# The mixing branches of a two-layer decoder step as stopping routines between the large products

## The chip, the cores and the metric

The kernel runs on one core of one Trainium2 chip. The metric is the device time of one execution in microseconds. Five engines work side by side, each through its own list of instructions in order: PE (TensorE, the matmuls), DVE (VectorE), ACT (ScalarE), POOL (GpSimd) and SP (SyncE, which here only issues DMA transfers). They wait for one another by semaphores. Matmuls write to eight PSUM banks; DVE and ACT read the banks out.

## What is computed

One inference step of a trunk of two layers. The rows (columns of x in the kernel) are 8 sequences of 4 new tokens with past state, and one prompt of 16 meta and 512 further tokens. Per layer:

```python
x = x + 0.5 * swiglu(rmsnorm(x, ffn1_norm), ffn1_w_in, ffn1_w_out)
h = rmsnorm(x, mix_norm)
fq, fk, fv, ff, sz, sxbc, sdt, gq, gk, gv, glr, gg = split(h @ w_mix_in)
# FoX: softmax attention on normalised q and k, bias = sums of log forget gates
# SSD: causal conv over x, B, C; state space recurrence in chunks of 128; gate silu(z); grouped norm
# GLA: linear attention with a decay per key channel from a low-rank gate; norm; swish gate
x = x + concat(fox_o, ssd_o, gla_o) @ w_mix_out
x = x + 0.5 * swiglu(rmsnorm(x, ffn2_norm), ffn2_w_in, ffn2_w_out)
```

The prompt attends causally to itself; the 8 sequences attend to 512 past tokens each, in pages of 128 that a page table names. New keys, values, gates and states are returned too.

## The kernel before

x lies in SBUF with 1024 features on 8 x 128 partitions and 560 columns. Group A is 304 columns (tile 4: 32 sample and 16 meta columns; tiles 0 and 1: 128 prompt columns each), group B 256 (tiles 2 and 3). Every large product is float32 by three terms: activations and weights are split into a high and a low part (`hhiA`, `hloA`, `whi`, `wlo`; A or B is the group), and `mm3` issues high x high, low x high and high x low for each of 8 pieces of the contraction: 24 matmuls in a row. `unit` fetches a 128 x 1024 piece of weights by a DMA on SP into one of three `raw` buffers, splits it in two halves on ACT (`whi`) and DVE (`wlo`, every fifth on POOL); there are four buffers of each.

A layer is ffn1, mix, ffn2. The two ffn parts are long rows of products. `mix` holds the rest: projections (`gla_in`, `fox_in`, `ssd_in`, per group), then for each tile the routines `gla_tile`, `ssd_tile`, `fox_tile`, for the sample columns `fox_decode` with 64 paged keys and values per layer, `fox_norm` for q and k, `fox_meta` (layer 0 only), then `split_o` (the branches' output O into high and low), `mix_out` (8 products per group and the sum into x) and the norm. In a tile, small matmuls alternate with steps on DVE, ACT and POOL. `ssd_tile` begins with products on `da`, transposes of the conv outputs `xc`, products of `s` (c_tri times dr) with c_strict, forms the weights `s` from them, multiplies them with the inputs, updates the state `Ssd` by a product with `sbt`, and at its end normalises y, with a diagonal matrix `dg` from ACT on the one side of a matmul, into O. The tiles of one branch hang on one another by the state.

The order in which the instructions are written decides on each engine's order. In `mix` it is a string, `MIX_ORDER` (line 162): every word calls the next stretch, up to a `yield`, of a projection, a tile's routine as a whole, a split, a part of `mix_out`. The scheduler of the framework then lets small matmuls slip between products where it sees room. `after(n, f)` delays a closure until n more products have been written. PSUM: 2 banks `psg` for products, 3 `psL` for GLA and SSD, 3 `psF` for FoX and the rest.

Of the kernel before, what the change touches and what calls it, by code (L numbers as in the profile page):

```python
# [173 lines left out]
BUFS = {"s1": 5, "f2": 3, "g2": 8, "s2": 5, "pg": 9}  # L174
# [58 lines left out]
class Trunk:  # L233
    def __init__(self, tc, a, es):
# [11 lines left out]
        self.pending = []  # L246
        self.nlo, self.lo_pool = 0, 0
# [23 lines left out]
    def mm(self, out, lhsT, rhs, start=True, stop=True, **k):  # L271
        return self.T.matmul(out, lhsT, rhs, start=start, stop=stop, **k)  # L272

    def tr(self, out, in_):
        p = in_.shape[0]
        self.T.transpose(out, in_, self.c("ident")[:p, :p])  # L276
# [157 lines left out]
    def mm3(self, out, parts):  # L434

        n = len(parts)
        for i, ((wh, wl), (xh, xl)) in enumerate(parts):
            self.mm(out, wh, xh, start=i == 0, stop=False)
            self.mm(out, wh, xl, start=False, stop=False)
            last = self.mm(out, wl, xh, start=False, stop=i == n - 1)  # L440
        self.tick(last)

    def after(self, n, f):

        self.pending.append([n, f])

# [206 lines left out]
    def fox_in(self, l, H):  # L653
# [20 lines left out]
        yield  # L674
        qa = self.qaug
        pst = self.ps(self.psF)
        for name in ("fk0", "fk1", "fq0", "fq1"):
            if name == "fq0":
                yield
            w = self.unit(self.a["wfm"][l, FMI[name]])  # L680
            isq, hp = name[1] == "q", int(name[2])
            for g in GRP:
# [8 lines left out]
                def sums(g=g, sq=sq, i=i, last=name == "fq1" and g == "B"):  # L691
                    for j, (ti, c0, tn) in enumerate(TILES[g]):
                        o = 8 * j + i + (24 if g == "B" else 0)
                        self.mm(pst[:, o:o + 2], sq[:, c0:c0 + 128], self.c("fsel"))
                    if last:
                        for h in GRP:
                            o, nt = 24 if h == "B" else 0, len(TILES[h])
                            self.V.tensor_scalar(self.R[h]["fst"][:, :nt, :], pst[:, o:o + 8 * nt].rearrange("p (j i) -> p j i", j=nt),
                                                 EPS, None, op0=ALU.add)
# [4 lines left out]
    def gla_in(self, l, g, H):  # L704
        R, n, nt = self.R[g], GRP[g][1], len(TILES[g])
        gin = self.g2(128 * nt).rearrange("p (j c) -> p j c", j=nt)
        pt = self.ps(self.psF)

        def use(j, ti, c0, tn, ps):
# [6 lines left out]
            self.tr(pt[:, 128 * j:128 * j + 128], gv[:, 0:128])  # L716

        self.tok_unit(l, 0, g, H, use)
        gt = self.g2(128 * nt)
        self.act(gt, pt[:, :128 * nt])  # L720
        pg = self.ps(self.psF)
        for j in range(nt):
            self.mm(pg[:, 128 * j:128 * j + 128], gt[:, 128 * j:128 * j + 128], self.wgate)
        self.tt(gin, pg[:, :128 * nt].rearrange("p (j c) -> p j c", j=nt), self.row["gb"].unsqueeze(1).to_broadcast([128, nt, 128]), ALU.add)
        self.log_sigmoid(gin.rearrange("p j c -> p (j c)"), self.g2(128 * nt), self.g2(128 * nt))
        gh = R["gh"] = self.t([128, 384], "gh", F32R)[:, :128 * nt].rearrange("p (j c) -> p j c", j=nt)
        gl = R["gl"] = self.t([128, 384], "gl", F32R)[:, :128 * nt].rearrange("p (j c) -> p j c", j=nt)
        self.act(gh, gin)
        self.tt(gl, gin, gh.bitcast(F32), ALU.subtract)
        yield  # L730
# [3 lines left out]
        yield  # L734
        for name in ("gg0", "gg1"):
# [3 lines left out]
            self.stt(t[:, :n], t[:, :n], 1.0, ps, ALU.add, ALU.mult)  # L739

    def ssd_in(self, l, g, H):
# [24 lines left out]
        for f in (4, 5, 0, 1, 2, 3):  # L766
            if f in (4, 1):
                yield
            self.conv(l, g, f, self.fm_unit(l, f"c{f}", g, H))
        yield  # L770
        self.tok_unit(l, 3, g, H, lambda *a: use(*a, half=1))

# [46 lines left out]
    def fox_norm(self, l, g):  # L819
# [7 lines left out]
        for j, (ti, c0, tn) in enumerate(tiles):  # L827
            e = self.f2(512)
            self.act(e.rearrange("p (h d) -> p h d", h=8), y[:, j, :].unsqueeze(2).to_broadcast([128, 8, 64]))
            ps = self.ps(self.psF)  # L830
# [26 lines left out]
        for j in range(3):  # L857
            self.tt(lw[:, 1, 4 * j + 4:4 * j + 8], lw[:, 1, 4 * j:4 * j + 4], lw[:, 0, 4 * j:4 * j + 4], ALU.add)
        ps = self.ps(self.psF)
# [26 lines left out]
    def diag(self, r, n):  # L886

        d = self.t([128, 128], "dg", bufs=2)[:n, :n]
# [3 lines left out]
    def fox_tile(self, g, i, c0):  # L892

        R = self.R[g]
# [3 lines left out]
        po = self.ps(self.psF)  # L898
        for hp in range(2):
            ets = []  # L900
            for h in (2 * hp, 2 * hp + 1):
# [16 lines left out]
                dg = self.diag(sums[:, 0:1], 128)  # L918
                pt = self.ps(self.psF)
                for k in range(i + 1):  # L920
                    o = 16 + 128 * k
                    self.mm(pt[:, 128 * k:128 * k + 128], e[0][:, o:o + 128] if o < nk else e[1], dg)
                et = self.f2(kc)
                self.V.tensor_copy(et, pt[:, :kc]) if h % 2 else self.act(et, pt[:, :kc])

# [3 lines left out]
                self.act(emt, pm[:, :128]) if h % 2 else self.V.tensor_copy(emt, pm[:, :128])  # L929
                ets.append((et, emt))  # L930

            for k in range(i + 2):
                for h2, (et, emt) in enumerate(ets):
                    d = slice(128 * hp + 64 * h2, 128 * hp + 64 * h2 + 64)
                    o = po[64 * h2:64 * h2 + 64, 128 * hp:128 * hp + 128]
# [123 lines left out]
    def ssd_tile(self, l, g, j, ti, c0, n):  # L1059
# [122 lines left out]
        if ti == 3:  # L1182
            self.store("ossmp", l, self.Ssd)
# [380 lines left out]
```

## Time and profile before

| | |
|---|---|
| time, median of 3 runs | 2401.96 us (2398.37 to 2403.77) |
| the profiled execution | 2399.53 us, its span 2397.4 us |
| mean granted clock of PE | 0.994 |
| PE busy | 2338.7 us (98%), 18041 matmuls |
| DVE / ACT / POOL busy | 1221.3 / 869.3 / 516.4 us |
| mix of layer 0 | 429.7 to 800.1 us |
| mix of layer 1 | 1622 to 1995 us |
| loaded from HBM | 219.47 MB, 95 GB/s over the span |

Times in the profile are microseconds from the start of the span. A row of instructions names engine, line, operation, output <- inputs and shape; L272 is the matmul helper, L276 the transpose, L279 a two-operand step, L282 one with a scalar besides, L285 an activation or copy on ACT. A wait is put down to the engine and tile that released it. Matmuls overlap in the pipeline, so their pace is the distance of their starts, not their duration. PEclk is the granted clock as a share of 2.4 GHz.

### The profile page before, as it was taken

What the parts mean: (1) busy time and instruction counts of PE and PEld (TensorE: products, weight loads), DVE (VectorE), ACT (ScalarE), POOL (GpSimd) and SP (SyncE); (2) the same over time, 40 slices, a digit from 0 to 9 for tenths busy, and PEclk for the clock granted to TensorE, in tenths of its full rate; (3) what the DMA queues carried; (4) which work ended last, traced back from release to release, by engine and by line L of the source; (5) the groups of instructions that cost most, each with busy time, mean ns of one, the idle gap of its engine ahead of it and who ended that gap; (6) DMA issues with size and microseconds to landing.
All of it is one profiled execution on the core that took longest, in us unless ns stands there. A gap on an engine that the chain in (4) does not pass through costs nothing.

```text
span 2397.4 us, 45049 instructions
## 1 busy us (share of the span) xinstructions
PE 2338.7 (98%) x18041; PEld 2251.5 (94%) x18041; DVE 1221.3 (51%) x2610; ACT 869.3 (36%) x1892; POOL 516.4 (22%) x696
## 2 busy tenths in 40 slices
PE   8999999999999999999999999999998999999999
PEld 8999999987788999999999999999877889999999
DVE  6434444477787633333353333344877975333333
ACT  5323223444455432322343232235444554323231
POOL 4202112334232310100131010113333323101010
PEclk9999999999999999999999999999999999999999
DMA  4222223335332322222322222233442323222222
GB/s 150 90 89 83 85 89 106 86 105 170 102 99 68 115 89 82 87 88 85 92 73 87 88 83 86 88 98 95 120 157 92 98 77 114 88 89 87 89 86 86
DMA packets 89762, 230.25 MB, mean 96 GB/s; under 512 B 12834, under 2 KB 38130, under 8 KB 89554
## 3 DMA queue, kind: packets, MB, share of 16 engines
q1 hardware_dynamic: 89122, 227.22, 30.5%
q8 instruction: 142, 2.33, 0.4%
q14 instruction: 66, 0.54, 0.1%
q10 hardware_dynamic: 432, 0.16, 0.0%
HBM read 219.47 MB, written 7.85 MB: 95 GB/s over the span
## 4 chain that ended last, share of the span: by engine, by line
PE 86%; DVE 7%; POOL 3%; ACT 2%; issue 2%; DMA 1%; POOLq 0%; DVEq 0%; ACTq 0%
PE ps L272 85%; DVE s L282 1%; POOL s L279 1%; DVE g L279 1%; DVE s L279 1%; PE ps L276 1%; DVE wlo L279 1%; DMA raw<-wout 1%; ACT s L285 1%; POOL gst L317 0%; POOL hloA L279 0%; DVE qaug L282 0%; ACT hhiA L285 0%; ACT whi L285 0%; DVE kaug L282 0%
## 5 line engine op out<-in xcount | busy, mean ns | idle before, releaser
L279 DVE TENSOR_TENSOR wlo<-raw,whi 128x512 fp32r<-128x512 f32 (+1 forms) x649 | 459.9, 711 | 400.7 <-ACT whi L285 391.0
L285 ACT ACTIVATE whi<-raw 128x512 fp32r<-128x512 f32 (+1 forms) x680 | 426.4, 630 | 609.3 <-PE ps L272 558.8
L272 PE MATMUL ps<-hhiA,whi 128*128 128x304 f32 (+1 forms) x1664 | 503.4, 303 | 0.0
L272 PE MATMUL ps<-hloA,whi 128*128 128x304 f32 (+1 forms) x1664 | 502.6, 302 | 0.0
L272 PE MATMUL ps<-hhiA,wlo 128*128 128x304 f32 (+1 forms) x1664 | 501.2, 301 | 0.0
L272 PE MATMUL ps<-hhiB,whi 128*128 128x256 f32 x1664 | 471.0, 283 | 3.7 <-ACT s L285 2.3
L272 PE MATMUL ps<-hhiB,wlo 128*128 128x256 f32 x1664 | 471.5, 283 | 1.9 <-DVE wlo L279 1.9
L272 PE MATMUL ps<-hloB,whi 128*128 128x256 f32 x1664 | 468.5, 282 | 0.0
L272 PEld LDWEIGHTS ps<-hhiB,whi 128*128 128x128 f32 x1664 | 315.4, 190 | 6.3 <-ACT s L285 4.3
L272 PEld LDWEIGHTS ps<-hhiB,wlo 128*128 128x128 f32 x1664 | 315.6, 190 | 3.2 <-DVE wlo L279 2.7
L272 PEld LDWEIGHTS ps<-hloA,whi 128*128 128x128 f32 x1664 | 314.2, 189 | 3.3 <-issue 2.4
L272 PEld LDWEIGHTS ps<-hloB,whi 128*128 128x128 f32 x1664 | 314.8, 189 | 1.9 <-issue 1.2
L272 PEld LDWEIGHTS ps<-hhiA,whi 128*128 128x128 f32 x1664 | 313.5, 188 | 1.8 <-issue 1.5
L272 PEld LDWEIGHTS ps<-hhiA,wlo 128*128 128x128 f32 x1664 | 313.7, 189 | 1.3 <-issue 0.8
L279 POOL TENSOR_TENSOR hidA<-s,hidA 128x304 fp32r<-128x304 f32 (+1 forms) x88 | 75.9, 863 | 824.4 <-ACT hidA L285 824.0
L272 PE MATMUL ps<-hidA,whi 128*128 128x304 f32 (+1 forms) x1072 | 223.4, 300 | 0.0
L282 DVE SCALAR_TENSOR_TENSOR x<-ps,x 128x304 f32<-128x304 f32 (+2 forms) x192 | 85.5, 447 | 233.8 <-PE ps L272 232.1
L272 PE MATMUL ps<-hidB,whi 128*128 128x256 f32 x1072 | 193.9, 281 | 0.0
L272 PEld LDWEIGHTS ps<-hidA,whi 128*128 128x128 f32 x1072 | 173.6, 188 | 0.0
L272 PEld LDWEIGHTS ps<-hidB,whi 128*128 128x128 f32 x1072 | 166.2, 189 | 0.0
L272 PE MATMUL ps<-hidA,wlo 128*128 128x304 f32 (+1 forms) x536 | 161.0, 300 | 0.0
L279 DVE TENSOR_TENSOR s<-s,ps 128x256 f32<-128x256 f32 (+4 forms) x194 | 89.9, 464 | 136.1 <-PE ps L272 127.7
(337 smaller groups left out, 3546.4 us busy)
## 6 DMA issues: line engine op xcount, KB each, us to landing
raw<-win SPq DMA_DIRECT2D x176, 512.0 KB, 3.5
raw<-wout SPq DMA_DIRECT2D x64, 512.0 KB, 3.5
raw<-wfm SPq DMA_DIRECT2D x48, 512.0 KB, 3.5
raw<-wmo SPq DMA_DIRECT2D x32, 512.0 KB, 3.6
raw<-wout SPq DMA_DIRECT2D x32, 384.0 KB, 3.4
pg<-kpage SPq DMA_DIRECT2D x64, 130.0 KB, 2.4
pg<-vpage SPq DMA_DIRECT2D x64, 128.0 KB, 2.2
raw<-wtm SPq DMA_DIRECT2D x8, 544.0 KB
```

The lines of the kernel that those rows point to most:

```text
L272: return self.T.matmul(out, lhsT, rhs, start=start, stop=stop, **k)
L276: self.T.transpose(out, in_, self.c("ident")[:p, :p])
L279: return (eng or self.V).tensor_tensor(out=out, in0=a, in1=b, op=op)
L282: return self.V.scalar_tensor_tensor(out=out, in0=a, scalar=s, in1=b, op0=op0, op1=op1)
L285: return self.S.activation(out, in_, f, **k)
```

## The change

`MIX_ORDER` goes. The projections are written in the order gla_in A, fox_in, ssd_in A, gla_in B, ssd_in B. Tiles become generators that `yield` an estimated number of microseconds at each point where PE would wait for another engine. Three lanes (G: GLA tiles 4, 0, 1, then 2, 3; S: SSD likewise; F: fox_norm, decode, FoX tiles 0, 1, meta, 2, 3) hold them. `mm` and `tr` count an estimated PE time in `now`; after each half of a product and each product, `step` advances the lanes that are due, and issues what they write behind that product. The closing products of an SSD or GLA tile go to a list of `ends`, due 7 or 6 us later. `finish` runs lanes without products between where a later stage needs it: S ahead of ssd_in B until tile 1 has its weights, G ahead of gla_in B until tile 1's state is there, and everything at the end. `mix_out` of A is now one piece with the rest of tiles 2 and 3 beside it, then B is split and its products follow, and norm A comes after B's first two.

PSUM banks: `psL` has 6 and `psF` is the same pool. Of smaller things: FoX tiles 0 to 2 put the meta columns' product into the bank of the others, and one copy takes all; FoX's output is copied per pair of heads; the gate's transposes in gla_in go tile by tile, each behind the next product; SSD's diagonal has a tag `ds` of its own and both are made ahead; GLA's `kr` has its own buffer; page buffers are 8 for 9. The core of the diff, with some parts cut:

```diff
-MIX_ORDER = """
-fox_in:A fox_in:A ssd_in:A fox_in:A gla_in:A gla_in:A O:A gla_in:A fox_norm:A fox_norm:B gla:4 decode:A fox:0
-fox:4 gla:0 gla:1 fox:1 ssd_in:A ssd_in:A ssd_in:A ssd:4 ssd:0 ssd:1 gla_in:B gla_in:B gla_in:B ssd_in:B
-ssd_in:B ssd_in:B ssd_in:B split:A O:B gla:2 fox:3 ssd:2 gla:3 out:A out:A fox:2 ssd:3 out:A split:B out:A
-out:B norm:A out:B out:B out:B norm:B
-"""
+STAGES = ("glaA", "fox", "ssdA", "glaB", "ssdB")
+
+LANES = {"G": {"A": (4, 0, 1), "B": (2, 3)}, "S": {"A": (4, 0, 1), "B": (2, 3)}, "F": (0, 1, 4, 2, 3)}
...
-BUFS = {"s1": 5, "f2": 3, "g2": 8, "s2": 5, "pg": 9}
+BUFS = {"s1": 5, "f2": 3, "g2": 8, "s2": 5, "pg": 8}
...
     def mm(self, out, lhsT, rhs, start=True, stop=True, **k):
+        n = int(np.prod(rhs.shape[1:]))
+        self.now += n / 2400 + 0.0125 if rhs.dtype == F32R else max(0.111, n / 1200)
         return self.T.matmul(out, lhsT, rhs, start=start, stop=stop, **k)
...
             last = self.mm(out, wl, xh, start=False, stop=i == n - 1)
+            if i == n // 2 - 1:
+                self.step(last)
         self.tick(last)
+        self.step(last)
...
+    def step(self, last):
+
+        for lane in list(self.lanes.values()):
+            if lane["q"] and lane["due"] <= self.now:
+                with self.tc.issue_after(last.ins):
+                    self.advance(lane)
+        for e in [e for e in self.ends if e[0] <= self.now]:
+            if e[1] in self.O:
+                self.ends.remove(e)
+                with self.tc.issue_after(last.ins):
+                    e[2]()
+
+    def advance(self, lane):
+
+        g = lane["q"][0]
+        try:
+            lane["due"] = self.now + next(g)
+        except StopIteration:
+            lane["q"].pop(0)
+            lane["due"] = self.now
+
+    def end(self, g, wait, f):
+
+        self.ends.append((self.now + wait, g, f))
+
+    def finish(self, names, until=lambda: False):
+
+        while not until():
+            lanes = [self.lanes[n] for n in names if self.lanes[n]["q"]]
+            if not lanes:
+                break
+            lane = min(lanes, key=lambda v: v["due"])
+            self.now = max(self.now, lane["due"])
+            self.advance(lane)
...
-            self.tr(pt[:, 128 * j:128 * j + 128], gv[:, 0:128])
+
+            def turn():
+                pt = self.ps(self.psF)
+                self.tr(pt[:, :128], gv[:, 0:128])
+                self.act(gt[:, 128 * j:128 * j + 128], pt[:, :128])
+
+            self.after(1, turn)
...
         for f in (4, 5, 0, 1, 2, 3):
-            if f in (4, 1):
-                yield
             self.conv(l, g, f, self.fm_unit(l, f"c{f}", g, H))
-        yield
+        self.branch("S", [self.ssd_tile(l, g, *a) for i in LANES["S"][g] for a in self.tile_of(g, i)], 5.0)
         self.tok_unit(l, 3, g, H, lambda *a: use(*a, half=1))
+        R["zz"] = True
...
+            yield 3.0
+            while g not in self.O:
+                yield 1.0
+
+            po = self.ps(self.psF)
...
-        self.act(self.O[g][:, 0:2, self.ocols(g, c0, 128)[0]], po[:, 0:256].rearrange("p (a b) -> p a b", a=2))
+            self.act(self.O[g][:, hp, self.ocols(g, c0, 128)[0]], po[:, 0:128])
...
+        while "zz" not in R:
+            yield 1.0
...
-        pt = self.ps(self.psL)
-        for g2 in range(2):
-            dg = self.diag(r[:, g2:g2 + 1], n)
-            for f in (2 * g2, 2 * g2 + 1):
-                self.mm(pt[:, f * n:(f + 1) * n], y[:, 128 * f:128 * f + 128], dg)
+        dgs = [self.diag(r[:, g2:g2 + 1], n, "ds") for g2 in range(2)]
...
+        self.end(g, 7.0, turn)
...
+        for w in STAGES:
+            if w == "fox":
+                self.fox_in(l, H)
+            elif w[:3] == "ssd":
+
+                if w[3] == "B":
+                    self.finish("S", lambda: ("S", 1) in self.done)
+                self.ssd_in(l, w[3], H)
+            else:
+                if w[3] == "B":
+                    self.finish("G", lambda: ("G", 1) in self.done)
+                self.gla_in(l, w[3], H)
+        self.finish("SG", lambda: {("S", 1, "end"), ("G", 1, "end")} <= self.done)
+        self.finish("F", lambda: ("F", 4) in self.done)
+        self.finish_ends("A")
+        S = self.split_o("A")
+        out("B")
+        self.lo_pool = 0
+        for _ in self.mix_out(l, "A", S):
+            pass
+        self.finish("SGF")
+        self.finish_ends("B")
+        N = {}
+        S = self.mix_out(l, "B", self.split_o("B"))
+        next(S)
+        N["A"] = self.norm("A", self.col["g2"])
...
-            with tc.tile_pool(name=f"mx{l}", bufs=1) as self.mx, ps(f"pl{l}", 3) as self.psL, ps(f"pf{l}", 3) as self.psF:
+            with tc.tile_pool(name=f"mx{l}", bufs=1) as self.mx, ps(f"pl{l}", 6) as self.psL:
+                self.psF = self.psL
```

Three places in PE's list, layer 0. The first is the start of the mix, after the transposes of the norm of group B (`c_ident,nr`); `gv` is the gate's input from gla_in. Before:

```order
L272 MATMUL ps_4978<-whi_4911,hloA_4759 128x260
L276 MATMUL ps_5003<-c_ident_80,nr_4972 128x128 x2
L272 MATMUL ps_5043<-whi_4897,hhiB_5006 128x260
L272 MATMUL ps_5043<-wlo_4898,hhiB_5006 128x260
L272 MATMUL ps_5043<-whi_4897,hloB_5007 128x260
```

and now:

```order
L272 MATMUL ps_4974<-whi_4906,hloA_4759 128x272
L277 MATMUL ps_4999<-c_ident_80,nr_4966 128x128 x2
L277 MATMUL ps_5036<-c_ident_80,gv_771_4972 128x128
L272 MATMUL ps_5052<-hhiA_4758,whi_5044 128x304
L272 MATMUL ps_5052<-hloA_4759,whi_5044 128x304
L272 MATMUL ps_5052<-hhiA_4758,wlo_5045 128x304
```

The first product on hhiB stood right behind the transposes; now products on A's columns follow.

The second is SSD tile 0 and the beginning of tile 1 (`s` times `c_strict_r`, `Ssd`, `sbt`, then `da` of the next tile). Before, around the closing products with `dg`, among products of z (shape 128x264):

```order
L272 MATMUL ps_8152<-wlo_8106,hhiB_5006 128x264
L272 MATMUL ps_8152<-whi_8105,hloB_5007 128x264
L272 MATMUL ps_8152<-whi_8109,hhiB_5006 128x264
L272 MATMUL ps_7748<-dg_7749,s_1311_7685 128x128 x2
L272 MATMUL ps_7748<-dg_7753,s_1311_7685 128x128 x2
L272 MATMUL ps_7758<-da_5370,c_tri_488 128x8
L272 MATMUL ps_7758<-da_5370,c_strict_r_490 128x8
L272 MATMUL ps_7758<-da_5370,c_ones_82 128x8
L276 MATMUL ps_7767<-c_ident_80,xc_1213_7250 128x128
```

and now, where the lane is finished ahead of ssd_in B:

```order
L272 MATMUL ps_7830<-s_1323_7823,c_strict_r_490 128x512
L272 MATMUL ps_7830<-s_1324_7825,c_strict_r_490 128x512
L272 MATMUL ps_7836<-s_1288_7718,s_1322_7820 128x64 x4
L272 MATMUL ps_7846<-Ssd_71,scz_7726 128x256 x2
L272 MATMUL ps_7836<-s_1288_7718,s_1327_7833 128x64 x4
L272 MATMUL ps_7854<-s_1331_7852,sbt_7724 64x256 x2
L272 MATMUL ps_7871<-da_6103,c_tri_488 128x8
L272 MATMUL ps_7871<-da_6103,c_strict_r_490 128x8
L272 MATMUL ps_7871<-da_6103,c_ones_82 128x8
L277 MATMUL ps_7880<-c_ident_80,xc_1038_6341 128x128
L277 MATMUL ps_7880<-c_ident_80,xc_1055_6418 128x128
```

The closing products are no longer between the two tiles, and no product stands between the second strict product of tile 0 and the transposes of tile 1.

The third is the end of the mix, with the last SSD tile's closing products. Before, among the products of out A (`hhiA`, `hloA`):

```order
L272 MATMUL ps_9339<-dg_9340,s_1724_9275 128x128 x2
L272 MATMUL ps_9449<-hloA_8565,whi_9441 128x304
L272 MATMUL ps_9449<-hhiA_8564,wlo_9442 128x304
L272 MATMUL ps_9339<-dg_9344,s_1724_9275 128x128 x2
L272 MATMUL ps_9155<-f_1715_9242,Vt_183_988 64x128
L272 MATMUL ps_9155<-f_1706_9221,Vt_184_989 64x128
L272 MATMUL ps_9155<-f_1715_9242,Vt_184_989 64x128
L272 MATMUL ps_9155<-f_1706_9221,Vt_185_990 64x128
L272 MATMUL ps_9155<-f_1715_9242,Vt_185_990 64x128
L272 MATMUL ps_9155<-femt_9225,Vm_992 64x128
L272 MATMUL ps_9155<-femt_9246,Vm_992 64x128
L272 MATMUL ps_9449<-hhiA_8564,whi_9441 128x304
```

and now:

```order
L272 MATMUL ps_9437<-hhiA_8755,wlo_9434 128x304
L272 MATMUL ps_9509<-hhiB_9481,whi_9501 128x256
L272 MATMUL ps_9415<-dg_9354,f_1734_9348 128x128 x3
L272 MATMUL ps_9415<-dg_9354,f_1735_9350 128x128
L272 MATMUL ps_9422<-dg_9354,f_1734_9348 128x128
L272 MATMUL ps_9462<-f_1748_9409,Vt_183_988 64x128
L272 MATMUL ps_9475<-ds_9400,s_1662_9092 128x128 x2
L272 MATMUL ps_9475<-ds_9402,s_1662_9092 128x128 x2
L272 MATMUL ps_9509<-hloB_9482,whi_9501 128x256
L272 MATMUL ps_9462<-f_1752_9420,Vt_183_988 64x128
L272 MATMUL ps_9462<-f_1748_9409,Vt_184_989 64x128
```

They now stand behind the first product of out B (`hhiB`), whose other operands are split from what they and the FoX products write.


## Rows read from the trace of the kernel before

**Rows 1.** The page: busy time of the engines; transfers of key pages.

```profile
PE 2338.7 (98%) x18041; PEld 2251.5 (94%) x18041; DVE 1221.3 (51%) x2610; ACT 869.3 (36%) x1892; POOL 516.4 (22%) x696
...
pg<-kpage SPq DMA_DIRECT2D x64, 130.0 KB, 2.4
```

**Rows 2.** Stretches: length, busy time of each engine, clock, DMA share, GB/s.

```profile
870.00:900.00 30.00, 30.00 (x236) 30.00 (x235) 10.84 (x20) 9.12 (x19) 4.43 (x5) 1.00 0.30 89
429.70:800.10 370.40, 350.81 (x2661) 308.22 (x2661) 276.32 (x698) 180.04 (x453) 123.82 (x194) 0.99 0.37 109
630.00:700.00 70.00, 63.13 (x447) 56.14 (x446) 64.86 (x141) 37.56 (x97) 28.15 (x35) 0.98 0.34 100
1622.00:1995.00 373.00, 348.57 (x2639) 306.74 (x2638) 276.06 (x690) 178.90 (x449) 125.14 (x194) 0.98 0.36 108
```

**Rows 3.** PE's waits in the mix of layer 0: total us, times, longest.

```profile
PE ps L272 <- ACT s L285: 3.4, 3, 1.7
...
PE ps L272 <- ACT dg L285: 1.8, 2, 1.0
...
PE ps L272 <- ACT hhiB L285: 1.0, 1, 1.0
...
PE ps L272 <- POOL hloB L279: 0.3, 1, 0.3
```

**Rows 4.** PE's waits in the mix of layer 1.

```profile
PE ps L272 <- ACT dg L285: 4.0, 3, 2.7
PE ps L276 <- DVE g L279: 2.5, 3, 1.1
```

**Rows 5.** Stretches at half clock, columns as in rows 2.

```profile
442.49:445.90 3.41, 3.41 (x16) 3.41 (x17) 2.76 (x9) 1.63 (x5) 2.98 (x4) 0.50 0.00 0
...
633.63:637.05 3.42, 3.42 (x16) 3.24 (x15) 3.38 (x5) 1.18 (x3) 2.52 (x2) 0.50 0.26 108
...
1828.30:1835.13 6.83, 6.71 (x28) 6.33 (x29) 1.64 (x5) 2.37 (x9) 1.47 (x1) 0.50 0.22 77
```

**Rows 6.** Timeline of PE, start of the mix, layer 0: start, duration, operands.

```profile
441.92 0.28 PE L272 MATMUL ps<-whi,hhiB 128*128 128x260 f32 x1
442.04 0.28 PE L272 MATMUL ps<-wlo,hhiB 128*128 128x260 f32 x1
...
442.72 0.42 PE L272 MATMUL ps<-whi,hhiB 128*128 128x260 f32 x1
442.94 0.42 PE L272 MATMUL ps<-wlo,hhiB 128*128 128x260 f32 x1
```

**Rows 7.** Timeline of PE, opening of SSD tile 0, layer 0: its first small matmuls.

```profile
631.37 0.39 PE L272 MATMUL ps<-da,c_tri 128*128 128x8 f32 x2
```

**Rows 8.** Timeline of PE, a run of products ending at small matmuls.

```profile
541.72 0.30 PE L272 MATMUL ps<-hloA,whi 128*128 128x304 f32 x1
541.86 0.30 PE L272 MATMUL ps<-hhiA,wlo 128*128 128x304 f32 x1
542.16 0.29 PE L276 MATMUL ps<-c_ident,g 48*128 48x48 f32 x2
```

**Rows 9.** Timeline of PE, end of SSD tile 0, layer 0.

```profile
644.50 0.28 PE L272 MATMUL ps<-whi,hhiB 128*128 128x264 f32 x1
644.71 0.65 PE L272 MATMUL ps<-s,sbt 128*64 128x256 f32 x4
...
649.36 1.16 PE L272 MATMUL ps<-dg,s 128*128 128x128 f32 x8 [1.02 <-ACT dg L285]
```

**Rows 10.** DVE's groups in the mix of layer 0, by shape: busy, mean ns.

```profile
L279 DVE TENSOR_TENSOR wlo<-raw,whi 128x512 fp32r<-128x512 f32 x75 | 53.9, 722 | 8.6 <-ACT whi L285 8.1
L282 DVE SCALAR_TENSOR_TENSOR s<-s,pder,s 128x256 f32<-128x256 f32 x18 | 11.6, 644 | 0.3 <-ACT s L285 0.3
L279 DVE TENSOR_TENSOR s<-c_tri,dr 128x512 fp32r<-128x512 f32 x8 | 9.1, 1133 | 0.0
...
L279 DVE TENSOR_TENSOR hloB<-O,hhiB 128x256 fp32r<-128x256 f32 x8 | 3.6, 496 | 1.0 <-ACT hhiB L285 1.0
```

More of the change, by code (lines that the diff above doesn't have):

```diff
@@ L246, in __init__ @@
         self.pending = []
+        self.lanes, self.ends, self.now = {}, [], 0.0
         self.nlo, self.lo_pool = 0, 0
@@ L275, in tr @@
         p = in_.shape[0]
+        self.now += 0.109
         self.T.transpose(out, in_, self.c("ident")[:p, :p])
@@ L739, in gla_in, with tile_of, branch @@
             self.stt(t[:, :n], t[:, :n], 1.0, ps, ALU.add, ALU.mult)
+        R["gg"] = True
+    def tile_of(self, g, i):
+        return [(j, ti, c0, n) for j, (ti, c0, n) in enumerate(TILES[g]) if ti == i]
+    def branch(self, name, gens, wait=0.0):
+        self.lanes[name]["q"] += gens
+        self.lanes[name]["due"] = max(self.lanes[name]["due"], self.now + wait)
     def ssd_in(self, l, g, H):
@@ L939, in fox_tile, with fox_way @@
                         self.mm(o, self.Vm[:, d], emt, start=False, stop=True)
-        self.act(self.O[g][:, 0:2, self.ocols(g, c0, 128)[0]], po[:, 0:256].rearrange("p (a b) -> p a b", a=2))
+            self.act(self.O[g][:, hp, self.ocols(g, c0, 128)[0]], po[:, 0:128])
+    def fox_way(self, l):
+        for g in GRP:
+            yield from self.fox_norm(l, g)
+        yield from self.fox_decode(l)
+        for i in LANES["F"]:
+            if i == 4:
+                if l < L - 1:
+                    yield from self.fox_meta()
+                self.done.add(("F", 4))
+                yield 0.0
+                continue
+            g = "A" if i < 2 else "B"
+            yield from self.fox_tile(g, i, *[c0 for ti, c0, n in TILES[g] if ti == i])
     def fox_meta(self):
@@ L1171, in ssd_tile @@
             V.tensor_scalar(bt_own, bt, self.c("tailcol")[:n], None, op0=ALU.mult)
+        if last:
+            yield 2.0
         pn = self.ps(self.psL)
@@ L1328, in gla_tile @@
                 self.tt(zm[:, q2], zr[:, :, 0:48], sm4[:, q2, :].unsqueeze(1).to_broadcast([128, 4, 48]))
+        yield 8.0 if last else 3.0
+        po = self.ps(self.psL)
+        if not last:
+            self.mm(po[:n, 0:256], zc, self.Sgl, stop=False)
         for h in range(4):
@@ L1378, in gla_tile, with turn @@
                 r.unsqueeze(2).to_broadcast([n, 4, 64]))
-        pt = self.ps(self.psL)
-        for hp in range(2):
-            self.tr(pt[:, hp * n:(hp + 1) * n], on[:, 128 * hp:128 * hp + 128])
         os, m = self.ocols(g, c0, n)
-        for hp in range(2):
-            self.stt(self.O[g][:, 6 + hp, os], pt[:, hp * n:hp * n + m], self.col["gn"], R[f"gg{hp}"][:, c0:c0 + m], ALU.mult, ALU.mult)
+        def turn():
+            pt = self.ps(self.psL)
+            for hp in range(2):
+                self.tr(pt[:, hp * n:(hp + 1) * n], on[:, 128 * hp:128 * hp + 128])
+            for hp in range(2):
+                self.stt(self.O[g][:, 6 + hp, os], pt[:, hp * n:hp * n + m], self.col["gn"], R[f"gg{hp}"][:, c0:c0 + m], ALU.mult, ALU.mult)
+        while "gg" not in R:
+            yield 1.0
+        self.end(g, 6.0, turn)
+        self.done.add(("G", ti, "end"))
+        yield 0.0
     def ocols(self, g, c0, n):
@@ L1425, in mix @@
         self.R = {"A": {}, "B": {}}
-        self.O, S, N = {}, {}, {}
-        run, live = {}, {}
-        for g in GRP:
-            for j, (ti, c0, n) in enumerate(TILES[g]):
-                run["gla", ti] = lambda a=(l, g, j, ti, c0, n): self.gla_tile(*a)
-                run["ssd", ti] = lambda a=(l, g, j, ti, c0, n): self.ssd_tile(*a)
-                run["fox", ti] = (lambda a=(g, ti, c0): self.fox_tile(*a)) if ti < 4 else self.fox_meta if l < L - 1 else lambda: None
-            run["gla_in", g] = lambda g=g: self.gla_in(l, g, H)
-            run["fox_in", "A"] = lambda: self.fox_in(l, H)
-            run["ssd_in", g] = lambda g=g: self.ssd_in(l, g, H)
-            run["fox_norm", g] = lambda g=g: self.fox_norm(l, g)
-            run["split", g] = lambda g=g: S.update({g: self.split_o(g)})
-            run["out", g] = lambda g=g: self.mix_out(l, g, S[g])
-            run["norm", g] = lambda g=g: N.update({g: self.norm(g, self.col["g2"])})
-            run["O", g] = lambda g=g: self.O.update({g: self.t([128, 8, 304], "O")[:, :, :self.grp[g][1]]})
@@ L1441, in mix @@
-        run["decode", "A"] = lambda: self.fox_decode(l)
-        for w in MIX_ORDER.split():
-            a, b = w.split(":")
-            self.lo_pool = 0 if a == "out" else LO_POOL
-            if w not in live:
-                live[w] = run[a, int(b) if b.isdigit() else b]()
-            if live[w] is not None:
-                next(live[w], None)
+        self.O, self.done = {}, set()
+        for n in LANES:
+            self.lanes[n] = {"q": [], "due": 0.0}
+        out = lambda g: self.O.update({g: self.t([128, 8, 304], "O")[:, :, :self.grp[g][1]]})
@@ new lines, in mix @@
+        self.finish("F", lambda: ("F", 4) in self.done)
[11 more added lines that the diff above has]
+        N["A"] = self.norm("A", self.col["g2"])
+        for _ in S:
+            pass
+        N["B"] = self.norm("B", self.col["g2"])
```

136 lines of the change are left out of this document (85 added, 51 removed).

## The prediction

> **What bounds the kernel now.** First the page: PE is busy 2338.7 of the span's 2397.4 us, DVE, next, only 1221.3 [rows 1]. So the question is where PE is not running at its pace. The table of stretches answers it: in a feed-forward stretch PE is busy 30.00 of 30.00 us, in the mix of layer 0 350.81 of 370.40, of layer 1 348.57 of 373.00 [rows 2]. The two mixes therefore hold 19.6 + 24.4 = 44.0 us of recorded PE idle, and only they are touched by the change. DVE is the second engine there: over the whole mix 276 of 370 us, but 64.86 of 70 us where the projections of B meet the SSD tiles (630 to 700) [rows 2].
>
> The list of PE's waits shows no single cause: in layer 0 the largest is for ACT's s with 3.4 us, that for ACT's dg 1.8; in layer 1 dg has 4.0 and DVE's g 2.5 [rows 3, 4]; some fifteen more follow in each. All are short chains inside one branch (a product of a tile, a step on ACT or DVE, the next product), in which PE stands because its next row is the chain's.
>
> The second loss is the clock. It falls to 0.50 (1.2 GHz) in five stretches, the first at 442.49, the last at 1828.30; three last 3.41 us and two 6.83 [rows 5], 23.9 us in all. Before 442.49 PE had waited 1.0 and 0.3 us for hhiB and hloB [rows 3]; there products start every 0.12 us at the full clock and 0.22 at half [rows 6]. So 45% of 23.9 us is lost: 10.8 us. Before the fall at 633.63 no wait is recorded, only the small matmuls that open SSD tile 0 from 631.37 on [rows 7].
>
> The third loss is changing between kinds. From the last product of a run to a following small matmul pass 0.30 us, where products are 0.14 apart [rows 8]: 0.16 a change at most; before the sbt products at 644.71 it is 0.21 [rows 9] against 0.12 [rows 6].
>
> **The change, part by part.** Both programs have the same products and small matmuls; what moves is their order.
>
> *Order of projections.* gla_in of A comes first, then fox_in. The first products on B's columns now stand behind some 22 us of A's, so the waits for hhiB (1.0 us) and hloB (0.3) go [rows 3]; both rows stand in layer 1 with the same numbers: 2.6 us. The fall at 442.49, which came behind them, goes too: 0.45 x 3.41 = 1.5. New there: each tile's gate transpose waits for ACT's copy of gv, but after the next product. Sum −4.1; bounds 0 (norm A's late parts take the place) and −5.
>
> *Routines in lanes.* What is left of the idle is 44.0 − 2.6 = 41.4 us. A step now comes due only after an estimated 2 to 8 us, behind a half product, and the closing products of a tile (dg, now ds) wait 7 us in the list of ends. Before, dg came 4.65 us after the state's product and PE still waited 1.02 us for it [rows 9]; behind the list that wait goes. If nothing new came, nearly all 41.4 would go. But DVE's work is the same and lies less evenly. Between the split of the second half of B's c4 weights and that of z1's first, DVE now has 91 rows: 18 conv steps at 0.644, seven weight splits at 0.722, four tri-times-dr steps at 1.133 make 21.2 us [rows 10], the other 62, at 0.35 each, some 22 (as DVE's 698 rows of the mix average 0.4 [rows 2]): 43 us. PE has 132 products there, at 0.12 us [rows 6] 15.8, and about 12.6 us of small matmuls: 28.4. Four buffers of split weights are two units, 5.8 us of products ahead. So PE waits some 9 us, an estimate. Counted the same way, conv A beside fox_norm (41.7 of DVE, 32.3 of PE) leaves 3.5. Third, the split of O for B now stands behind all of out A, with the last SSD and FoX products in the middle of out B's first two outputs: eight splits, DVE's half of them at 0.496 [rows 10], 4 us, of which out B's own first products cover 1: 3 us. 9 + 3.5 + 3 = 15.5 a layer, 31 in two, against 41.4: −10. Bounds: −31 (DVE keeps ahead) and +14 (rival D).
>
> *Clock.* The other four falls are 20.5 us, of which 45% are 9.2. The waits before them go in part, but the finish ahead of ssd_in B makes two SSD tiles run on with hardly a product between: from the last strict products of tile 0 to those of tile 1 are some 6.4 us of small matmuls, ten transposes among them; the fall at 633.63 too came behind the small matmuls of a tile's opening [rows 5, 7]. I let half return: −4.6, bounds −9.2 and +6. The Trainium skill, "TensorE: Matmul & The Clock Gate", section "Part 4: PE-mode transpose", says that transposes do not count as busy for the clock in the way that other matmuls do. By that rule the clock would fall in this stretch of each layer again and nothing of the 4.6 come in: the sum would be −16 and the time 2386. One fall does not tell whether the transposes of that opening or its 8-column products did it, so I keep half.
>
> *Fewer changes.* Products and small matmuls change 180 times a layer for 204 before: 48 fewer in two layers, at 0.09 to 0.16 us 4.3 to 7.7. Part of it is hidden in waits; I take −4, bounds 0 and −7.7.
>
> *Banks, pages, evacuations.* Six banks in one pool for three and three let G and S run on while decode holds two; at nothing by itself, since the largest waits [rows 3, 4] are those of a chain's own steps; were a bank late, it would cost what such a step does, about 1 us. Pages have eight buffers for nine; a page lands in 2.4 us [rows 1], and one buffer less can make a group of four late by that at the most: +1 a layer, bounds 0 and +2.4. The meta columns' own copies merge with the large ones, FoX's output is copied per head pair, gate transposes one by one: all on ACT and DVE at half load outside the crowd, cost nothing; if the crowd grows by them, tenths.
>
> Sum: −4.1 − 10 − 4.6 − 4 + 2 = −20.7. The profiled execution took 2399.53 us (span plus 2.1), 2.4 under the median of 2401.96. So 2379 for such a run and **2382** for the median.
>
> **The rivals.**
>
> *B, the waits really go.* DVE runs ahead far enough and the clock stays: of 44 + 10.8 + 6 = 61 us, some 12 stay (the split for B, the first steps of a tile), so −49: 2353. For it: before, DVE at 93% still let PE be busy 63.13 of 70 [rows 2]. Against it: the crowd is computed from the same DVE rows and is denser.
>
> *C, given back.* Idle moves into the crowd (DVE 5 us a layer more than I count) and the clock falls as often as before: −4.1 − 4 + 2 = −6 → 2396, or 2400 with a page late. The Trainium skill, "TensorE: Matmul & The Clock Gate", section "A second HAM failure mode: psum-queue depth-cycling", tells of a kernel that went round PSUM banks with tiny gaps between groups and whose clock swung between its levels. By that rule one pool of six banks that all branches turn through would keep all falls, which is this rival. The trace bears out the cause only in part: the fall at 442.49 followed gaps of 1.0 and 0.3 us [rows 3], that at 633.63 no recorded one.
>
> *D, slower: the SSD chains become the bound.* Before, tile 0 takes 631.37 to 644.71, 13.3 us from its first product to its state [rows 7, 9], with other work between. In the new order tiles 0 and 1 follow one another there, and nearly no product stands beside them: PE has about 24.5 us of rows, the chains need 2 x 13.3 = 26.6 at the old pace. If each of some ten DVE steps a tile meets one conv step or weight split (0.64 or 0.72) ahead of it, that is +7 a tile, 9 to 14 us of wait a layer, on which the half clock follows (0.45 x 6.83 = 3.1 a layer). It decides once the pair takes over 35 us; at 9 us a layer: +18 + 6 of wait and clock, −10 for what the rest gives (−4.1 − 4 − 2): +14 → 2416. For it: no steps of the program are left to lay between. Against it: G and FoX tiles are advanced in the same drain and fill some of the waits.
>
> *That the lanes do nothing* can be left out: the order of PE's rows differs from the start of the mix on.
>
> **How the numbers follow.** A change of 0.2% (4.8 us) is about what a measurement of this kernel can tell from none. Forecast A 0.45 (2372 to 2392 by its own bounds), B 0.15, C 0.16, D 0.24. Faster: A 0.42, B 0.15, C 0.04: 0.61. Same (2397 to 2407): A 0.03, C 0.10, D 0.02: 0.15. Slower: C 0.02, D 0.22: 0.24. The range leaves out the far half of D and a little of B: 2354 to 2412.
>
> **What would show it.** Right: mix idle near 15 us a layer; no wait for hhiB or dg among the largest; waits for wlo or conv's xc instead, in the six conv products of B; two or three falls of the clock rather than five; the split of B visible as a wait of PE for hhiB or hloB at the end. B: mixes of some 348 us each. D: from tile 0's first da product to tile 1's state product in the middle of B's projections over 35 us, with PE waiting for s. C: idle at 40 or more, or five falls. Wrong altogether: a feed-forward stretch that changes, or PE's small products themselves longer than before.

## The result and the profile after

The changed kernel takes 2427.76 us (2419.71 to 2432.70 over 4 runs), the kernel before 2402.17 beside it: 1.0106 times as long, 95% interval 1.0071 to 1.0140. It is 25.6 us slower, where 2382 was forecast; the range ended at 2412. The busy time of the engines in its profiled execution (2423.65 us), and three stretches of it, with the columns of [rows 2]:

```profile
PE 2342.0 (97%) x18041; PEld 2266.0 (94%) x18041; DVE 1219.3 (50%) x2610; ACT 865.1 (36%) x1894; POOL 523.8 (22%) x696
```

```profile
870.00:900.00 30.00, 30.00 (x236) 30.00 (x235) 10.87 (x20) 10.03 (x20) 4.41 (x6) 1.00 0.28 89
427.50:811.40 383.90, 351.80 (x2662) 314.89 (x2661) 276.07 (x698) 177.90 (x454) 127.84 (x194) 0.95 0.35 105
1634.70:2018.10 383.40, 351.16 (x2639) 315.27 (x2638) 274.23 (x689) 176.99 (x449) 128.49 (x194) 0.94 0.35 105
```

The feed-forward stretch is as it was. The two mixes are 13.5 and 10.4 us longer than in [rows 2], 23.9 in all. PE's idle in them is 32.1 + 32.2 = 64.3 us for 44.0, 20.3 more; its busy time is 3.6 more. The work on each engine is nearly the same. The waits of PE in the mix of layer 0 (columns as in [rows 3]):

```profile
PE ps L272 <- ACT s L286: 7.1, 2, 4.9
PE ps L272 <- DVE s L280: 3.7, 2, 2.3
PE ps L272 <- DVE dt L283: 3.5, 1, 3.5
PE ps L272 <- POOL s L280: 3.4, 3, 2.0
...
PE ps L272 <- DMA pg<-kpage: 1.7, 1, 1.7
```

and of layer 1:

```profile
PE ps L272 <- ACT s L286: 9.3, 2, 5.7
PE ps L272 <- DMA pg<-kpage: 5.5, 1, 5.5
PE ps L272 <- DVE dt L283: 3.5, 1, 3.5
```

Before, the longest wait was 1.7 us in layer 0 and 2.7 in layer 1; now six of 3.5 to 5.7 us make 26.6 of the 64.3. These six lie in three places: the products around conv A, the SSD pair (SSD tiles 0 and 1, which `finish` runs one behind the other ahead of ssd_in B), and the K pages. The clock fell too. Before it was at 1.2 GHz for 23.9 us in five stretches [rows 5], now for 88.8 in eleven. The first, and the longest of each layer, which lies in the SSD pair:

```profile
477.88:484.70 6.82, 6.82 (x28) 6.17 (x28) 1.76 (x7) 0.55 (x2) 1.47 (x2) 0.50 0.23 84
...
648.54:665.61 17.07, 11.29 (x41) 7.85 (x40) 11.82 (x36) 7.29 (x27) 7.47 (x7) 0.50 0.19 63
...
1867.10:1884.17 17.07, 11.12 (x40) 7.68 (x39) 12.28 (x37) 7.09 (x27) 7.64 (x7) 0.50 0.20 63
```

**Conv A.** PE, ACT and DVE of layer 0, from the timelines:

```profile
553.22 0.30 PE L272 MATMUL ps<-hloA,whi 128*128 128x304 f32 x1
558.38 0.45 PE L272 MATMUL ps<-whi,hhiA 128*48 128x256 f32 x1 [4.86 <-ACT s L286]
```

```profile
555.58 0.48 ACT L286 ACTIVATE s<-s 128x328 f32<-128x328 f32 x1 [1.79 <-DVE s L283]
557.93 0.40 ACT L286 ACTIVATE s<-ps 128x272 f32<-128x272 f32 x1 [1.88 <-DVE s L832]
```

```profile
554.65 0.42 DVE L280 TENSOR_TENSOR g<-ps,gst 128x256 f32<-128x256 f32 x1 [0.93 <-POOL gst L318]
...
555.46 0.47 DVE L283 SCALAR_TENSOR_TENSOR kaug<-kaug,pcol,ps 64x256 f32<-64x256 f32 x1
555.94 0.48 DVE L283 SCALAR_TENSOR_TENSOR qaug<-qaug,pder,ps 64x256 f32<-64x256 f32 x1
556.35 0.53 DVE L283 SCALAR_TENSOR_TENSOR xc<-s,s 128x32 f32<-128x32 f32 x2
556.80 0.48 DVE L283 SCALAR_TENSOR_TENSOR kaug<-kaug,pcol,ps 64x256 f32<-64x256 f32 x1
...
557.71 0.19 DVE L832 COPY s<-ps 128x32 f32<-128x32 f32 x1
```

Read from below: DVE's small copy of the conv's sample columns comes behind fox_norm's steps on qaug and kaug and a GLA step that itself waits for POOL; ACT's copy of the rest is behind it; only then is one of the two banks for products free, and PE has stood 4.86 us. In layer 1 the same wait is 5.7.

**The SSD pair.** The stretch from tile 0's first product to the end of tile 1's state product, after in both layers and, below, before in layer 0:

```profile
631.70:671.30 39.60, 30.16 (x175) 24.65 (x174) 31.84 (x75) 15.45 (x48) 14.83 (x14) 0.78 0.13 42
1849.30:1889.90 40.60, 31.74 (x172) 26.08 (x173) 29.81 (x74) 15.48 (x46) 13.67 (x14) 0.74 0.13 40
```

```profile
631.30:663.50 32.20, 29.64 (x196) 25.31 (x195) 28.39 (x48) 12.66 (x34) 13.69 (x13) 0.95 0.25 80
```

Before, PE idled 2.6 us there (4.1 in layer 1), now 9.4 and 8.9, at a mean clock of 0.78 and 0.74. Before, 94 products lay in the pair in layer 0, now 42. The longest wait of the pair, 3.48 us in either layer, is that of tile 1's first strict product; DVE and PE in layer 0:

```profile
650.59 0.68 DVE L280 TENSOR_TENSOR wlo<-raw,whi 128x512 fp32r<-128x512 f32 x1
...
651.47 0.68 DVE L280 TENSOR_TENSOR wlo<-raw,whi 128x512 fp32r<-128x512 f32 x1
652.07 0.68 DVE L280 TENSOR_TENSOR s<-s,dt 128x512 f32<-128x512 f32 x1
652.67 0.68 DVE L280 TENSOR_TENSOR s<-c_tri,dr 128x512 fp32r<-128x512 f32 x1
```

```profile
653.50 0.77 PE L272 MATMUL ps<-s,c_strict_r 128*128 128x512 f32 x1 [3.48 <-DVE dt L283]
```

The s that it multiplies is DVE's row at 652.67, behind two weight splits; the wait is put down to dt, DVE's next row.

### The profile page after: what moved, and what is told of

Same layout as the page of the kernel before. It is cut to its first block, busy times and chain, and to the rows that moved or that the text cites. A ratio compares the mean times of both kernels' runs of the same rounds, so it can differ in the third digit from the quotient of the medians.

```text
span 2421.8 us, 44988 instructions
## 1 busy us (share of the span) xinstructions
PE 2342.0 (97%) x18041; PEld 2266.0 (94%) x18041; DVE 1219.3 (50%) x2610; ACT 865.1 (36%) x1894; POOL 523.8 (22%) x696
## 4 chain that ended last, share of the span: by engine, by line
PE 61%; DVE 4%; DMA 2%; ACT 1%; POOL 1%; issue 1%; SPq 0%; DVEq 0%; POOLq 0%; ACTq 0%
PE ps L272 60%; DMA raw<-wout 2%; DVE wlo L280 1%; DVE s L280 1%; POOL s L280 1%; PE ps L277 0%; ACT keep L286 0%; DVE s L283 0%; DVE g L280 0%; DMA pg<-vpage 0%; ACT whi L286 0%; ACT s L286 0%; DVE g L283 0%; DVE keep L280 0%; DMA s<-sssm 0%
## 5 line engine op out<-in xcount | busy, mean ns | idle before, releaser
L280 DVE TENSOR_TENSOR wlo<-raw,whi 128x512 fp32r<-128x512 f32 (+3 forms) x649 | 467.0, 723 | 398.5 <-ACT whi L286 390.3
L272 PE MATMUL ps<-hhiA,whi 128*128 128x304 f32 (+1 forms) x1664 | 510.6, 307 | 9.0 <-ACT s L286 5.9
```

The lines of the kernel that those rows point to most:

```text
L280: return (eng or self.V).tensor_tensor(out=out, in0=a, in1=b, op=op)
```

## The experiments

Each is timed against the kernel before on the same chip; "2401.6 (0.9988)" gives the median and the ratio. Three theories stood at first: the SSD pair lies bare since the finish ahead of ssd_in B drains the lanes (1); conv A's steps meet fox_norm's on DVE (2); six shared banks make the branches wait for each other's (3). Two came with the runs: free banks let small matmuls be set ahead of the products that should cover them (4), and the hold, by which `step` issues a lane's rows behind a fixed product (`issue_after`), makes PE wait.

**Which part costs: order, banks.** e1, in the changed kernel, puts the projections of SSD first and those of FoX third:

```diff
-STAGES = ("glaA", "fox", "ssdA", "glaB", "ssdB")
+STAGES = ("ssdA", "glaA", "fox", "ssdB", "glaB")
```

> The changed kernel with the projections in the order ssd_in A, gla_in A, fox_in, ssd_in B, gla_in B: some 57 us of products now lie between conv A and ssd_in B, and fox_norm no longer falls beside conv A. Theory 1 (the SSD pair finished ahead of ssd_in B): its 12 us of wait and 17 us of half clock a layer go, 15 to 20 us a layer, unless FoX is late at the end, which shows as a run of FoX products without large products ahead of out A. Theory 2 (DVE's crowd of conv A and fox_norm): the waits of 7 to 10 us a layer in the products of conv A go, 15 to 20 us in all, and the half clock at the SSD pair stays. Theory 3 (shared banks): nothing moves, 2425. Price of FoX being late, not known: up to 30 us a layer.

2456.1 us (1.0212, 1.0186 to 1.0237). The edit brought its unknown price with it: FoX is late, and from 715 to 741 us of layer 0 PE has only FoX's chains, with 1.5 to 1.7 us of wait before each set of dg products. So its time decides nothing on theories 1 and 2. Its trace says more: in the pair lie 208 and 209 products, and PE idles 0.3 and 1.4 us there, so the wait went as theory 1 has it. Around conv A, now first in the mix and without fox_norm beside it, PE still waits 4.9 and 5.8 us for ACT's s.

e2, in the changed kernel, gives the branches three and three banks again:

```diff
-            with tc.tile_pool(name=f"mx{l}", bufs=1) as self.mx, ps(f"pl{l}", 6) as self.psL:
-                self.psF = self.psL
+            with tc.tile_pool(name=f"mx{l}", bufs=1) as self.mx, ps(f"pl{l}", 3) as self.psL, ps(f"pf{l}", 3) as self.psF:
```

> The changed kernel with three banks for GLA and SSD and three for FoX and the rest, as before. Theory 3 (a branch waits for a bank of the shared pool that a slow branch holds): 10 us or more faster. Theories 1 and 2: no faster; a few us slower, since SSD and GLA now share three banks in the pair.

2401.6 us (0.9988, 0.9952 to 1.0023): 26.2 under the changed kernel. Theory 3's number came, though not its reason (e9). The four executions lie far apart, 2393.08, 2395.43, 2407.70 and 2409.81, all below the 2419.71 that the changed kernel took at the least; the trace is of the third. In the pair lie 81 products now, and PE is busy more:

```profile
629.00:671.10 42.10, 37.20 (x248) 31.03 (x247) 35.97 (x77) 19.47 (x61) 15.02 (x15) 0.92 0.29 98
```

PE's idle in the pair falls to 4.9 and 5.3 us, and the half clock from 88.8 to 71.7. The longest waits around conv A are the same 4.9 and 5.7.

e3 gives the kernel before the new order of projections, in `MIX_ORDER`:

```diff
-fox_in:A fox_in:A ssd_in:A fox_in:A gla_in:A gla_in:A O:A gla_in:A fox_norm:A
+gla_in:A gla_in:A O:A fox_in:A fox_in:A ssd_in:A fox_in:A gla_in:A fox_norm:A
```

> The kernel before, its order written by hand, with gla_in A ahead of fox_in and nothing else changed: the waits for hhiB go. My sum gives 3 to 4 us faster (2398). If the order of projections is what costs, it is 10 us or more slower.

2425.0 us (1.0080, 1.0051 to 1.0108), 21.4 slower. The waits for hhiB went, but fox_norm came to stand behind fox_in with two products between, and its chain on DVE and POOL lies open:

```profile
521.59 0.62 PE L272 MATMUL ps<-c_tri,f 128*128 128x128 f32 x4 [1.14 <-POOL g L1323]
526.79 0.58 PE L272 MATMUL ps<-c_ones,f 128*128 128x128 f32 x1 [4.58 <-DVE f L279]
```

In both layers a stretch of 20.48 us at half clock follows there. My sum of −4.1 counted what the new place takes away, not what gla_in A had covered in the old one.

e4 gives the kernel before the six shared banks:

```diff
-            with tc.tile_pool(name=f"mx{l}", bufs=1) as self.mx, ps(f"pl{l}", 3) as self.psL, ps(f"pf{l}", 3) as self.psF:
+            with tc.tile_pool(name=f"mx{l}", bufs=1) as self.mx, ps(f"pl{l}", 6) as self.psL:
+                self.psF = self.psL
```

> The kernel before with six banks in one pool for three and three and nothing else changed. Theory 3: slower by 5 us or more. Otherwise within 4 us of 2402.

2605.9 us (1.0834, 1.0808 to 1.0860): 202 us from a line that I had put at nothing. The largest wait is for dg, an operand that ACT makes, and not for a bank; in layer 0:

```profile
PE ps L272 <- ACT dg L285: 27.8, 13, 6.4
PE ps L272 <- DVE s L279: 8.7, 6, 2.8
PE ps L272 <- DVE g L279: 5.6, 5, 2.8
```

In the SSD pair lie 21 products for 94. With the pool shared, small matmuls are set ahead of the products that covered their waits.

**Is it sharing, or the number?** e7 (two and four) and e9 (`ps(f"pl{l}", 4)`, shared):

> The changed kernel with two banks for GLA and SSD and four for FoX and the rest. Theory 4 (free banks let small matmuls be set ahead of the products that should cover them): fewer banks for SSD keep more products between its steps; within 6 us of 2402 on either side. If SSD needs three banks for its chain: slower by 10 us or more.

2405.4 us (1.0018, 1.0003 to 1.0034), within 6 us of three and three, with 87 products in the pair. SSD does not need its third bank much.

> The changed kernel with four banks in the shared pool for six (two banks of PSUM unused in the mix). Theory 4 (the more banks are free, the further small matmuls are set ahead of the products that should cover them): faster than with six, 2402 to 2415. Theory 3 (in a shared pool a branch waits for banks that another holds): slower than with six, 2440 or more. PE's list differs from that with six in few rows; if only the rows of the SSD pair matter, the waits of 3.9 and 2.5 us there are what goes.

2410.9 us (1.0040, 1.0023 to 1.0056): 17 faster than with six, as theory 4 has it. Theory 3 falls: had branches waited for each other's banks, fewer would have been slower. But the pair has 41 products, no more than with six, and from its first product to the start of tile 1's state product it is shorter all the same, 37.5 and 33.8 us for 38.7 and 40.2. So two pools keep products between the steps, of whatever size (81 with three and three, 87 with two and four), and one pool does not, with four banks or six; what four banks give, they give in another way. In the pair of the changed kernel DVE took GLA's steps ahead of SSD's:

```profile
637.53 2.76 DVE L280 TENSOR_TENSOR g<-g,gqm 128x256 f32<-128x256 f32 x3
...
641.41 0.68 DVE L280 TENSOR_TENSOR s<-c_tri,dr 128x512 fp32r<-128x512 f32 x1
```

and PE's next strict products, at 642.24, had waited 2.27 us for that s. This is not it: in layer 0 of e9 the same steps of GLA stand ahead, and PE waits 1.85. Over both mixes its PE idles some 9 us less, and the half clock is 68.3 us for 88.8; where the 17 us come from stays open.

**DVE beside conv A.** e5 (fox_in first, three and three banks, `branch("F", ..., 12.0)`), e6 and e15:

```diff
-            yield 2.5 if j else 5.0
+            yield 4.5 if j else 5.0
```

> The changed kernel with three and three banks and fox_in ahead of gla_in A, as before the change (FoX's lane starts 12 us later so that fox_norm finds its sums). Theory 2 (fox_norm beside conv A crowds DVE: waits of 5.0, 2.5, 5.9 and 3.8 us there with either set of banks): fox_norm falls beside gla_in A, these waits go, 12 to 17 us; the waits for hhiB (2.6 in two layers) come back; 2385 to 2392. If conv A is slow by itself (its own 24 steps a group on DVE): the waits stay, about 2404.

2395.9 us (0.9983, 0.9971 to 0.9996): 5.7 under e2, and short of the 2385 to 2392 expected. The waits of 5 us at conv A are gone, but one of 3.3 comes at fox_norm in layer 1.

> The changed kernel with three and three banks and 4.5 us for 2.5 between the tiles of fox_norm. Theory 2: its ten qaug and kaug steps lie thinner over conv A, the waits of 5.0 and 2.5 us halve: 5 to 10 us faster than 2402. If not: 2402, or a few us slower since the pages' decode starts some 8 us later.

2397.0 us (0.9994, 0.9968 to 1.0020): 4.6 under e2, just short of what was expected, and e2's own executions spread over 17 us. With these two alone the theory is not settled.

> The changed kernel (six shared banks, all held) with 4.5 us for 2.5 between the tiles of fox_norm and nothing else. With three and three banks this gave 4.6 us. If DVE's crowd costs as predicted (3.5 us a layer) or as its waits show (7.5 and 9.6): 5 to 15 us faster than 2428, and the waits of 5.0 and 5.9 us before a z product of A go. If the banks hide it: 2428.

2414.0 us (1.0052, 1.0035 to 1.0069): 13.8 under the changed kernel by this one number, as expected. The largest wait for ACT's s in layer 0 falls from 4.9 to 2.4; in layer 1 that of 5.7 falls to 0.9, but one of 4.8 comes at the next z product. All waits for ACT's s together fall only from 16.4 to 13.1 us, and the half clock from 88.8 to 68.3. Theory 2 is borne out in its sign; how much of the 13.8 is the crowd on DVE, and how much the clock, is not shown.

**The hold behind a product.** e8 (three and three) and e10 (six shared) drop it in `step`, for the lanes and for the closing products; e13 drops it for lane F alone, e14 for lanes S and G, and both keep it for the closing products:

```diff
-                with self.tc.issue_after(last.ins):
+                if True:
                     self.advance(lane)
...
-                with self.tc.issue_after(last.ins):
+                if True:
                     e[2]()
```

> The changed kernel with three and three banks; what step() advances is no longer held behind the product it follows (no issue_after in step). If the driver's placing is what gains against the order by hand, PE's small matmuls move ahead of products and it is slower by 5 us or more; if the scheduler places them as well, 2402 within 4.

2391.0 us (0.9961, 0.9948 to 0.9973): 10.5 faster than e2, the opposite of what I expected, though e2's spread leaves the size open. With the hold, a K page's products stand behind a fixed product and PE waits for the DMA, as in e2's layer 1:

```profile
1784.97 0.29 PE L272 MATMUL ps<-whi,hloB 128*128 128x272 f32 x1
1790.51 1.08 PE L272 MATMUL ps<-pg,qbd 128*32 128x128 f32 x16 [5.25 <-DMA pg<-kpage]
```

Without it no wait for a K page is left in the list, and that of conv A falls to 0.9 us; the longest are now 3.5 and 3.8, for a step of FoX on DVE.

> The changed kernel with its six shared banks, and what step() advances not held behind its product. If the cost of the shared pool and that of the hold add up: 2428 - 10 = 2417. If the hold is what makes the shared pool costly: near 2391, as with three and three. If the shared pool without the hold lets the rows run ahead as in the kernel before with one pool: above 2450.

2402.8 us (1.0000, 0.9988 to 1.0012): 25 faster than held, and 11.7 slower than e8; none of the three numbers expected. By the medians the two parts make each other worse: sharing costs 26.2 with the hold, 11.7 without.

> Three and three banks; only FoX's lane is not held behind its product, SSD's and GLA's are (their closing products too). If the hold costs by PE standing at K pages that have not landed (5.2 us at one product of layer 1): near 2391, as with no hold at all, and that wait is gone. If it costs by SSD's and GLA's rows: 2402.

2397.4 us (0.9979, 0.9965 to 0.9994), its runs from 2387.7 to 2405.7. The waits went as the first of the two expectations has it, kpage to none and ACT's s to 1.6 and 2.8 us, but only 4 of the 10.5 us came.

> Three and three banks; only FoX's lane (and the closing products) is held, SSD's and GLA's are not. If the pages are the cause: 2400 to 2402, the wait for kpage in layer 1 stays at about 5 us. If SSD's and GLA's rows are: near 2391.

2401.6 us (0.9991, 0.9981 to 1.0001), as e2. FoX's hold keeps both waits; here in layer 1:

```profile
PE ps L272 <- ACT s L286: 5.9, 1, 5.9
PE ps L272 <- DMA pg<-kpage: 4.4, 1, 4.4
```

So those waits are FoX's hold, and freeing SSD and GLA alone gives nothing. Why freeing FoX alone gives only part stays open; the closing products, held in e13 and e14 and free in e8, were not tried by themselves, and e13's trace still has 61.4 us at half clock, e8's 47.8.

**Together.** e11 is e5 without the hold, e12 is e6 without it, e16 has all three edits:

> Three and three banks, no hold behind products, fox_in ahead of gla_in A (the lane 12 us later). If the two gains add up (10.5 and 5.7 of 2401.6): 2385. If both mend the same waits (conv A beside fox_norm): 2391 to 2396.

2388.9 us (0.9942, 0.9924 to 0.9960): between the two numbers expected, and 2.1 under e8 where fox_in first gave 5.7 with the hold; neither is decided.

> Three and three banks, no hold behind products, 4.5 us for 2.5 between the tiles of fox_norm. If the gains add up (10.5 and 4.6): 2386. If both mend the waits in conv A: 2391.

2385.3 us (0.9930, 0.9906 to 0.9954): 17.4 under the kernel before, 42.5 under the changed one. That is what adding up would give, and 5.7 under e8. Its mixes, 358.9 and 364.2 us for 370.4 and 373.0 before:

```profile
429.30:788.20 358.90, 341.23 (x2661) 304.47 (x2660) 274.34 (x698) 178.10 (x454) 125.75 (x194) 0.99 0.38 113
1610.10:1974.30 364.20, 343.11 (x2622) 304.33 (x2620) 271.97 (x687) 173.60 (x446) 119.09 (x192) 0.97 0.37 110
```

> Three and three banks, no hold, fox_in ahead of gla_in A and 4.5 us between the tiles of fox_norm. If the cures are of different waits: below 2385. If of the same: 2385 to 2389.

2386.5 us (0.9937, 0.9920 to 0.9954): with fox_in first as well nothing more comes, as expected where both mend the same waits.

The best version is the change with three and three banks, no hold in `step`, and 4.5 us between the tiles of fox_norm: faster than both kernels.

## Why the prediction was wrong

The view of what bounds the kernel held: the mixes alone changed, and the idle and the clock there decided. By its steps:

*Banks, pages, evacuations* was the step that failed most. It put six shared banks "at nothing by itself", since the largest waits were those of a chain's own steps. They cost 26.2 us (e2), 11.7 without the hold (e10 for e8), and 202 in the kernel before (e4). The two pools had been a brake on the order: with them the scheduler sets products between the steps of a chain (81 in the pair, 94 before), with one pool it sets the chains' rows one behind the other (42 and 21). That is only part of the cost: four shared banks leave as few products in the pair and still give 17 of the 26 back (e9), and why is open. That the largest waits before were not for banks did not mean that the banks did nothing: they held back rows that would have waited. The pages, put at 1 us a layer, cost 1.7 and 5.5 of wait for kpage, by the hold and not by the ninth buffer: without the hold eight buffers leave none (e8) to 0.9 (e12).

The hold had no term in the sum at all. It costs 25 us with six shared banks (e10), and some 10 with three and three, less surely (e8). With two pools alone the change is still 20 us over the forecast (e2); with the hold gone and fox_norm spread as well it is at 2385.3 (e12). That this is near the forecast 2382 (2381 by its own sum) is luck, since its other terms came out otherwise.

*Order of projections*, −4.1: the waits for hhiB went as said, 2.6 us, and the fall at 442.49 too. Uncounted was what gla_in A had covered behind fox_in: alone the new order costs 21.4 (e3). In the changed kernel conv A covers fox_norm instead, at the price of the next step.

*Routines in lanes*, −10: the 31 us of remaining waits became 64.3 us of idle. Conv A was put at 3.5 us a layer; its two largest waits make 7.1 and 9.3. The crowd at conv B, put at 9 a layer, leaves under 2. The split for B, put at 3, costs 0.3 in layer 0 and nothing in layer 1; the split for A, put at nothing, costs 3.9 in layer 0, with 6.8 us of half clock behind it. The SSD pair, left to rival D, idles 9.4 and 8.9. That dg's waits go was right: 0.3 is left for SSD's.

*Fewer changes*, −4: by the starts of PE's rows, products and small matmuls change 367 times in the two mixes for 417, as counted. What that gave can't be read from the runs.

*Clock*, −4.6: it went the other way, from 23.9 to 88.8 us at half clock, far past its bound of +6. What that cost can't be split off the idle: PE's busy time grew by 3.6 us only. The rule in "Part 4: PE-mode transpose" of the Trainium skill's "TensorE: Matmul & The Clock Gate" had nothing of the 4.6 come in. The trace agrees so far that each pair, ten transposes in it, has its long fall (the prediction has all ten between the strict products, where five are). But the same ten stand in the pairs before and in e2, with 3.4 to 6.8 us at half clock for 17.07, and PE was busy only 11.29 of those 17.07. So the transposes alone do not set the length; a row of them without waits was not tested. The bank cycling of rival C agrees in direction: without the hold the half clock is 58.0 us with the one pool of six (e10) and 47.8 with three and three (e8), with the hold 88.8 and 71.7. The hold moves it too, and no run turns through the banks without changing the waits, so it is neither shown nor excluded as a cause.

Rival D named the sign and one of the places with its mark (a pair over 35 us; it took 38.7 and 40.2), with 0.24 and 2416. Its mechanism, SSD's steps on DVE behind weight splits, is in the wait of 3.48 us. Its 9 us a layer are the idle there, of which 6.9 and 4.8 are new; conv A and the pages came on top. Its claim that the drain alone does it is not borne out: with three and three banks the drain stays, the pair takes 41 to 44 us, and PE works in it.

## What to carry to other kernels

Separate pools of buffers can be what keeps a static order good: before pooling banks, look at what a branch would now put ahead of the work that covers it. Before moving a stage, ask what it covers where it stands, not only what waits for it. When rows are held behind a fixed instruction of another stream, price that hold, above all for rows that depend on a DMA. Where the steps of two branches meet on one engine, try spreading one of them before moving it.

## What the runs showed of the hardware

With chains laid open in e4 the granted clock was 0.85 on average over the mixes for 0.99 and 0.98 before, its longest stretch at 1.2 GHz 61.44 us; in the best version it is 0.99 and 0.97. But the sum of PE's idle alone does not set it: from 400 to 2300 us PE idles 44.3 us before, 46.4 in e13 and 46.4 in e14, with 23.9, 61.4 and 78.5 us at half clock.

The time of one program spreads with nothing changed, and it goes with the granted clock. e2 took 2393.08 and 2395.43 us at a mean clock of 0.989, 2407.70 at 0.984 and 2409.81 at 0.981; e13's ten executions go from 2387.70 at 0.992 to 2405.71 at 0.985. From 0.989 to 0.981 is some 38 us more at half clock, of which 45% [rows 6] are 17 us, an estimate; measured are 16.7. Why the clock differs from one execution to the next no run shows.
